# Cut passes, permuted passes and single activation tiles in the feed-forward of a two-layer trunk

## The chip, the cores and the metric

The kernel runs on one core of one Trainium2 chip. The metric is the device time of one execution in microseconds. Three runs of the kernel before took 2742.55, 2743.82 and 2744.37 us; their median is 2743.82 us. One further execution was taken with the hardware profiler.

## The reference

A trunk of two layers works on 256 tokens of 2048 features in float32. Each layer has a mixer and a feed-forward, both with an RMS norm ahead and a residual behind. The mixer of layer 0 is differential attention, that of layer 1 a gated DeltaNet. The change lies in the feed-forward, which is the same in both layers:

```python
def conv_ffn(h, w_up, conv_w, conv_b, w_down):
    u = causal_dwconv(h @ w_up, conv_w) + conv_b
    val, gate = jnp.split(u, 2, axis=-1)
    return (jax.nn.silu(gate) * val) @ w_down

for i in range(DEPTH):                    # DEPTH = 2
    h = rms_norm(x, mixer_norm[i])
    x = x + (diff_attention(h, ...) if i == 0 else gated_deltanet(h, ...))
    x = x + conv_ffn(rms_norm(x, ffn_norm[i]), ffn_w_up[i], ffn_conv_w[i], ffn_conv_b[i], ffn_w_down[i])
```

`w_up` is 2048 x 11008 and `w_down` 5504 x 2048 in each layer. The causal convolution has three taps.

## The kernel before

Activations are kept transposed, features on the 128 partitions and the 256 tokens along the free dimension. `self.x` holds the residual as 16 tiles of 128 x 256, `self.h` the normed input of the next product.

Every large product is done in three passes. A float32 operand is split into a high part, rounded to the fp32r type, and a low part, the rest. ScalarE makes the high part of a weight chunk (L78), VectorE the low part (L79), both in `weights`; activations are split likewise in `norm_tile`, `split` and elsewhere, and stand as a tile of two halves, `a[:, 0]` high and `a[:, 1]` low. The three passes are high weights by high activations (L104, called h below), low weights by high activations (L105, m), and high weights by low activations (L106, l). They add into one PSUM bank.

`dense` (L90) makes one block of 256 output features: two columns c of 128, 16 or more contraction steps k, three passes for each pair of k and c, each a matmul of 128 x 128 weights by 256 tokens. The weights come in chunks of four k (CK = 4), 512 KB each, by a DMA from SP into `raw` (four buffers), and from there into `whi` and `wlo` (three buffers each). Within a chunk k runs outside c; in the last chunk of a block c runs outside k. After each chunk `tick` lets background generators (the norm's sum, attention scores, DeltaNet steps) issue their own instructions, so that their matmuls stand in TensorE's queue between those of `dense`. `dense_tok` (L125 to L127) is the variant with 512 columns, used for values and gates.

The feed-forward (`ffn`) runs 43 blocks j of the up projection, each with 16 k, so 96 passes a block and 4128 in all. Block j holds 128 value and 128 gate features. The block's sums go through `merge` (L112), the convolution, SiLU and the product on VectorE and ScalarE, and are split into the activation tile `ac` of block j. Then `project` runs eight blocks of the down projection with 43 k each, 2064 passes, whose activations are the `ac` tiles. At the start of each feed-forward, `norm_stat` is the one background generator: it adds matmuls of the plain float32 type, of 256 columns (L167) and one column (L169), near the start, and multiplies the inverse norm in at `merge`. Later no other matmul stands among the passes of a feed-forward.

Tiles come from pools in the order of their first allocation, rounded to 32 bytes. The constants' pool holds `h0` to `h15`, 2048 bytes each, and is followed by the pool of the weight buffers; the pools of attention, feed-forward and DeltaNet follow and replace each other. In the kernel before, three tiles carry unused columns at their ends: `dist` 72, `fcols` 64 and `con` 64. Modulo 512 bytes, all activations that `dense` reads (`h`, `ac` of attention, `ac` of the feed-forward, `oc` of the DeltaNet) then start at 160, and all weight buffers at 480.

The order of instructions on each engine is set by a scheduler when the program is built. It follows the order of the source closely; waits are put where regions that are read and written overlap.

Of the kernel before, what the change touches and what calls it, by code (L numbers as in the profile page):

```python
# [8 lines left out]
F32 = mybir.dt.float32  # L9
F32R = mybir.dt.float32r  # L10
# [6 lines left out]
P = 128  # L17
T = 256
D = 2048
KD = D // P  # L20
# [5 lines left out]
class Trunk:  # L26
# [8 lines left out]
    def __init__(self, ctx, tc):  # L35
        self.tc, self.nc = tc, tc.nc
        nc = self.nc
        self.bg = deque()
        self.cp = ctx.enter_context(tc.tile_pool(name="cp", bufs=1))
        self.wp = ctx.enter_context(tc.tile_pool(name="wp", bufs=2))  # L40
        self.sp = ctx.enter_context(tc.tile_pool(name="sp", bufs=2))
        self.dps = ctx.enter_context(tc.tile_pool(name="dps", bufs=2, space=PSUM))
        self.mps = ctx.enter_context(tc.tile_pool(name="mps", bufs=4, space=PSUM))
        self.ones = self.cp.tile([P, P], F32, tag="ones", name="ones")
        nc.vector.memset(self.ones, 1.0)
        self.eps = self.cp.tile([P, 1], F32, tag="eps", name="eps")
        nc.vector.memset(self.eps, EPS)
        self.x = self.cp.tile([P, KD, T], F32, tag="x", name="x")
        self.h = [self.cp.tile([P, 2, T], F32R, tag=f"h{k}", name=f"h{k}") for k in range(KD)]
        self.onesr = self.cp.tile([P, P], F32R, tag="onesr", name="onesr")  # L50
        nc.vector.tensor_copy(self.onesr, self.ones)
        self.squares = []
        self.ss = None
        nc.scalar.preload_act_table_set(LNEXP)

    def mp(self):
        return self.mps.tile([P, 512], F32, tag="mp", name="mp")
# [29 lines left out]
    def banks(self):  # L87
        return self.dps.tile([P, 2, 2 * T], F32, tag="ps", name="ps")

    def dense(self, w, kt, acts, tiles=2, lead=0):  # L90

        nc = self.nc
        ps = self.banks()
        for k0, nk in self.chunks(kt, CK, lead):
            hi, lo = self.weights(w[:, k0:k0 + nk, :])
            steps = [(k, c) for k in range(nk) for c in range(tiles)]
            if k0 + nk == kt:
                steps = [(k, c) for c in range(tiles) for k in range(nk)]
            for k, c in steps:
                a = acts(k0 + k)  # L100
                first, last = k0 + k == 0, k0 + k == kt - 1
                s = slice(c * P, (c + 1) * P)
                o = ps[:, c, :T]
                nc.tensor.matmul(o, hi[:, k, s], a[:, 0, :], start=first, stop=False)  # L104
                nc.tensor.matmul(o, lo[:, k, s], a[:, 0, :], start=False, stop=False)  # L105
                nc.tensor.matmul(o, hi[:, k, s], a[:, 1, :], start=False, stop=last)  # L106
            self.tick()
        return ps

# [127 lines left out]
    def ffn(self, w_up, w_down, nj, cols_ap, done, final=False):  # L237

        nc = self.nc
        self.spawn(self.norm_stat())  # L240
        with self.tc.tile_pool(name="fp", bufs=1) as fp:
            cols = fp.tile([P, 8 * nj + 64], F32, tag="fcols", name="fcols")[:, :8 * nj]
            cols = cols.rearrange("p (t h j) -> p t h j", t=4, h=2)
            nc.scalar.dma_start(cols, cols_ap)
            acts = []
            for j in range(nj):
                ps = self.dense(w_up[j], KD, self.h_acts)
                c = []
                u = fp.tile([P, 2, T], F32, tag="u", name="u", bufs=2)
                self.merge(ps, u)  # L250
                for half in range(2):
                    o = fp.tile([P, T], F32, tag=f"cv{half}", name="cv", bufs=2)
                    c4 = [cols[:, t, half, j:j + 1] for t in range(4)]
                    self.conv(o, u[:, half, :], c4[:3], c4[3])
                    c.append(o)
                nc.scalar.activation(c[1], c[1], AF.Silu)
                a = c[0]
                nc.vector.tensor_tensor(a, c[0], c[1], ALU.mult)
                ac = fp.tile([P, 2, T], F32R, tag=f"ac{j}", name="ac")
                self.split(ac, a)  # L260
                acts.append(ac)
            self.project(w_down, nj, lambda k: acts[k], done, final)
# [134 lines left out]
    def gdn(self, w_gate, w_in, w_z, w_out, nb, hb, gate_ap, const_ap, hot_ap, conv_col, ng, done):  # L397
# [7 lines left out]
        nc, tc, mp = self.nc, self.tc, self.mp  # L405
# [3 lines left out]
        gv = 2 * gh  # L409
        with tc.tile_pool(name="gd", bufs=1) as gd:  # L410
            self.spawn(self.norm_stat())
            con = gd.tile([P, 384 + 64], F32, tag="con", name="con")[:, :384]
            nc.sync.dma_start(con, const_ap)
            ident, mask, triu = con[:, :P], con[:, P:T], con[:, T:]
            hot = gd.tile([64, nv], F32, tag="hot", name="hot")
# [15 lines left out]
            def lin(ps):  # L431
                u = gd.tile([P, 2, T], F32, tag="u", name="u", bufs=2)
                self.merge(ps, u)
                return u

            def convs(u, tiles):
                c = gd.tile([P, 2, T], F32, tag="cv", name="cv", bufs=4)
                for i in range(2):
                    self.conv(c[:, i, :], u[:, i, :], [conv_col(t, tiles[i]) for t in range(4)], None)
                nc.scalar.activation(c, c, AF.Silu)  # L440
                return c
# [126 lines left out]
            def to_tokens(c, vt, g, ready):  # L568
                yield
                yield  # L570
                p = mp()
                for t in range(2):
                    for i in range(2):
                        nc.tensor.transpose(p[:, (2 * t + i) * P:(2 * t + i + 1) * P], c[:, i, t * P:(t + 1) * P], ident)  # L574
                nc.scalar.copy(vt[:, :, g:g + 2, :], p.rearrange("p (t v c) -> p t v c", t=2, v=2))
                ready.append(g)
# [70 lines left out]
            def out(b, acts):  # L647
                for blk in range(KD // 2):
                    ps = self.dense(w_out[b * (KD // 2) + blk], 2 * hb, lambda k: self.await_(acts, k))
                    self.add_out(blk, ps, done if b == nb - 1 else None)  # L650
# [4 lines left out]
            for b in range(nb):  # L655
                heads = range(b * hb, (b + 1) * hb)
                cc = gd.tile([P, 32, 32], F32, tag="s4", name="Cc", bufs=3)
                nc.gpsimd.memset(cc, 0.0)
                lqs, inv, acts, zts, vts = [], [], [], {}, {}
                groups = [range(i, i + gh) for i in range(0, hb, gh)]  # L660
                plan = [("k", i) for i in range(hb)] + [("v", 0)] + [("z", g) for g in range(len(groups))]
                for op, i in plan + [("v", i) for i in range(1, hb)]:
                    if op == "k":
                        hq = heads[i]
                        c = convs(lin(self.dense(w_in[hq * 2], KD, self.h_acts)), (hq, nq + hq))
                        self.spawn(keys(hq, c, cc, 2 * i, lqs))
                        if i == hb - 1:
                            self.spawn(invert(cc, lqs, inv))
                    elif op == "z":
                        gr = groups[i]  # L670
                        zt = zts[i] = gd.tile([P, 2, gv, P], F32, tag="vz", name="zt", bufs=4)
                        ps = self.dense_tok(w_z[heads[gr[0]] // 2], KD, self.h_acts)
                        for t in range(2):
                            nc.scalar.activation(zt[:, t].rearrange(flat), ps[:, t, :], AF.Silu,
                                                 scale=self.rstdc[:, t:t + 1])
                    else:
                        gi = i // gh
                        gr = groups[gi]
                        if i == gr[0]:
                            vt = gd.tile([P, 2, gv, P], F32, tag="vz", name="vt", bufs=4)  # L680
                            ready = []
                            self.spawn(group(gi, gr, lqs, inv, vt, ready, zts, acts))
                        hq = heads[i]
                        c = convs(lin(self.dense(w_in[hq * 2 + 1], KD, self.h_acts)),
                                  (2 * nq + 2 * hq, 2 * nq + 2 * hq + 1))
                        self.spawn(to_tokens(c, vt, 2 * (i - gr[0]), ready))
                if pend:
                    out(*pend)
                pend = (b, acts)
            out(*pend)  # L690

    def gates(self, gd, pg, nv, gp, ident, triu, res):
# [199 lines left out]
```

## Time and profile before

| | |
|---|---|
| median of three runs | 2743.82 us |
| lowest, highest | 2742.55, 2744.37 us |
| the profiled execution, its own time | 2744.12 us |
| its span, first to last instruction | 2742.3 us |
| granted TensorE clock, mean | 0.999 |
| matmul instructions in it | 22352, as many weight loads |
| passes of the two feed-forwards (L104, L105, L106) | 2 x 6192 |
| bytes moved by DMA | 481.62 MB, 176 GB/s on the mean |

The page gives for each engine the busy time and its share of the span. PE is TensorE's matmuls, PEld its weight loads, which overlap the matmuls; DVE is VectorE, ACT ScalarE. A matmul's drawn length is modelled and overlaps the next one's, so the time that one matmul costs is the distance between its start and the next start, read from the timeline. A window's row lists, for a stretch of the span, its length and for each engine the busy time and, in brackets, the number of instructions in it. A group's row lists line, engine, operation, the tiles written and read, shapes and count, then busy time and mean of one in ns, then the idle time before them and what ended it.

### The profile page before, as it was taken

The page shows a single profiled execution, that of the slowest core. Times are in us where ns is not written, and L with a number is a line of the kernel's source. Part 1 is how long each engine was busy: PE and PEld are TensorE (multiplying, and loading weights), DVE is VectorE, ACT ScalarE, POOL GpSimd, SP SyncE. Part 2 cuts the span into 40 slices and gives each one's busy share as a digit, 9 for nine tenths or more (in the row PEclk, how much of TensorE's full clock was granted, in tenths as well). Part 3 has the DMA queues.
Part 4 walks back from the last instruction along what each step waited for, and adds up shares of the span by engine and source line. Part 5 has one row for each costly group of instructions (what it writes and reads, how often), then busy time and mean ns, then how long its engine had stood idle before and what let it go on. Part 6 is the DMA issues. An engine that isn't in the chain of part 4 may idle for free.

```text
span 2742.3 us, 53669 instructions
## 1 busy us (share of the span) xinstructions
PE 2728.7 (100%) x22352; PEld 2656.1 (97%) x22352; DVE 1857.5 (68%) x2719; ACT 1457.5 (53%) x1994; POOL 118.4 (4%) x220
## 2 busy tenths in 40 slices
PE   8999999999999999999999999999999999999999
PEld 8998999999999999989989989989999999999999
DVE  7775667666666555688787787688676666665444
ACT  6565655555555444574764664574555555554333
POOL 0000000000000000021011011021000000000000
PEclk9999999999999999999999999999999999999999
DMA  6555555555555556545354454454455555556664
GB/s 214 169 169 169 168 189 185 186 188 188 186 186 189 185 187 187 186 155 177 122 170 140 147 172 144 155 168 157 152 187 186 186 187 188 186 186 193 191 196 151
DMA packets 135396, 481.62 MB, mean 176 GB/s; under 512 B 15344, under 2 KB 18416, under 8 KB 135152
## 3 DMA queue, kind: packets, MB, share of 16 engines
q1 hardware_dynamic: 134000, 475.57, 53.8%
q8 instruction: 175, 2.87, 0.4%
q10 hardware_dynamic: 1152, 2.61, 0.3%
q14 instruction: 69, 0.57, 0.1%
HBM read 476.03 MB, written 2.10 MB: 174 GB/s over the span
## 4 chain that ended last, share of the span: by engine, by line
PE 99%; ACT 0%; DVE 0%; DMA 0%; issue 0%; SPq 0%; DVEq 0%; ACTq 0%
PE ps L105 28%; PE ps L104 27%; PE ps L106 27%; PE ps L125 3%; PE ps L127 3%; PE ps L126 3%; PE mp L595 2%; PE mp L213 1%; PE mp L483 1%; PE mp L538 0%; PE mp L547 0%; PE mp L460 0%; PE mp L559 0%; PE mp L565 0%; PE mp L574 0%; PE mp L482 0%
## 5 line engine op out<-in xcount | busy, mean ns | idle before, releaser
L79 DVE TENSOR_TENSOR wlo<-raw,whi 128x1024 fp32r<-128x1024 f32 (+2 forms) x909 | 1108.5, 1220 | 690.1 <-ACT whi L78 685.4
L78 ACT CAST whi<-raw 128x1024 fp32r<-128x1024 f32 (+2 forms) x909 | 950.8, 1047 | 1091.3 <-PE ps L106 913.1
L104 PE MATMUL ps<-h,whi 128*128 128x256 f32 x4304 | 1208.2, 281 | 9.0 <-ACT h L139 5.3
L105 PE MATMUL ps<-h,wlo 128*128 128x256 f32 x4304 | 1209.1, 281 | 0.5 <-DVE wlo L79 0.4
L106 PE MATMUL ps<-h,whi 128*128 128x256 f32 x4304 | 1207.8, 281 | 0.0
L104 PEld LDWEIGHTS ps<-h,whi 128*128 128x128 f32 x4304 | 820.7, 191 | 11.6 <-ACT h L139 5.3
L105 PEld LDWEIGHTS ps<-h,wlo 128*128 128x128 f32 x4304 | 810.2, 188 | 4.3 <-DVE wlo L79 1.2
L106 PEld LDWEIGHTS ps<-h,whi 128*128 128x128 f32 x4304 | 809.9, 188 | 1.4
L104 PE MATMUL ps<-ac,whi 128*128 128x256 f32 x1632 | 458.4, 281 | 0.0
L105 PE MATMUL ps<-ac,wlo 128*128 128x256 f32 x1632 | 458.3, 281 | 0.0
L106 PE MATMUL ps<-ac,whi 128*128 128x256 f32 x1632 | 458.2, 281 | 0.0
L104 PEld LDWEIGHTS ps<-ac,whi 128*128 128x128 f32 x1632 | 312.2, 191 | 0.0
L105 PEld LDWEIGHTS ps<-ac,wlo 128*128 128x128 f32 x1632 | 307.2, 188 | 0.0
L106 PEld LDWEIGHTS ps<-ac,whi 128*128 128x128 f32 x1632 | 306.2, 188 | 0.0
L125 PE MATMUL ps<-whi,h 128*128 128x512 f32 x384 | 151.7, 396 | 0.0
L127 PE MATMUL ps<-whi,h 128*128 128x512 f32 x384 | 150.8, 393 | 0.0
L126 PE MATMUL ps<-wlo,h 128*128 128x512 f32 x384 | 150.6, 392 | 0.0
L104 PE MATMUL ps<-oc,whi 128*128 128x256 f32 x512 | 145.5, 284 | 0.0
L106 PE MATMUL ps<-oc,whi 128*128 128x256 f32 x512 | 145.0, 283 | 0.0
L105 PE MATMUL ps<-oc,wlo 128*128 128x256 f32 x512 | 144.8, 283 | 0.0
L194 DVE SCALAR_TENSOR_TENSOR cv<-u,fcols,cv 128x255 f32<-128x255 f32 (+1 forms) x344 | 142.8, 478 | 0.0
L112 DVE TENSOR_TENSOR u<-ps,rstd 128x512 f32<-128x512 f32 x118 | 81.4, 690 | 51.0 <-PE ps L106 50.9
(201 smaller groups left out, 2227.1 us busy)
## 6 DMA issues: line engine op xcount, KB each, us to landing
raw<-w_up SPq DMA_DIRECT2D x344, 512.0 KB, 4.3
raw<-w_down SPq DMA_DIRECT2D x160, 512.0 KB, 3.6
raw<-w_in SPq DMA_DIRECT2D x128, 512.0 KB, 4.3
raw<-w_z SPq DMA_DIRECT2D x64, 512.0 KB, 3.8
raw<-w_out SPq DMA_DIRECT2D x64, 512.0 KB, 3.6
raw<-w_qk SPq DMA_DIRECT2D x63, 512.0 KB, 4.0
raw<-w_v SPq DMA_DIRECT2D x32, 512.0 KB, 3.7
raw<-w_o SPq DMA_DIRECT2D x32, 512.0 KB, 4.3
```

The source lines that it names most:

```text
L78: nc.scalar.copy(hi, raw)
L79: nc.vector.tensor_tensor(lo, raw, hi.bitcast(F32), ALU.subtract)
L104: nc.tensor.matmul(o, hi[:, k, s], a[:, 0, :], start=first, stop=False)
L105: nc.tensor.matmul(o, lo[:, k, s], a[:, 0, :], start=False, stop=False)
L106: nc.tensor.matmul(o, hi[:, k, s], a[:, 1, :], start=False, stop=last)
L112: self.nc.vector.tensor_tensor(u, ps[:, :, :T], self.rstd.unsqueeze(1).to_broadcast([P, 2, T]), ALU.mult)
L125: nc.tensor.matmul(ps[:, c, :], ah, hi[:, k, :], start=first, stop=False)
L126: nc.tensor.matmul(ps[:, c, :], ah, lo[:, k, :], start=False, stop=False)
L127: nc.tensor.matmul(ps[:, c, :], al, hi[:, k, :], start=False, stop=last)
L194: nc.vector.scalar_tensor_tensor(out[:, j:], u[:, :T - j], taps[n - 1 - j], out[:, j:], ALU.mult, ALU.add)
L213: last = self.nc.tensor.matmul(out, self.onesr, p[:, j], start=i + j == 0, stop=i + j == n)
L595: nc.tensor.matmul(p[:, v, :], l(v), r[:, v, :], start=i == 0, stop=i == len(terms) - 1)
```

## The change

`dense` takes an order of the three passes and a column at which to cut. In layer 0 (not `final`), every second block has one pass cut: the high pass of k = 1, c = 0 becomes two matmuls, over tokens 0 to w and w to 256, with w = 2, 14, 26, ..., 230 in blocks 1, 3, ..., 39 and 254 in block 41. In layer 1 (`final`), block j takes one of seven orders by j modulo 7: hml, hlm, mhl, HML, hml, lhm, HLM. Lower case means that the three passes of one k and c follow each other in that order; upper case that both c are run for each pass of a k, in all chunks, before the next pass.

The tiles `h0` to `h15` become one tile with eight more columns (32 bytes), and the `ac` tiles of a feed-forward one tile with eight more columns, now allocated ahead of `u` and `cv`. `h` starts at column 0 up to the last output projection of the DeltaNet, where `place(4)` moves its rows by four elements (16 bytes) for layer 1's feed-forward; `ac` starts at column 4 in layer 0 and 0 in layer 1. The 64 unused columns of `con` go.

The built program has 21 matmuls more than before (21,586 in place of 21,565 in the source's counting). On the other engines the same instructions stand in the same order; the counts of matmuls that they wait for are shifted by the added matmuls, and by one or two more where an order lets a weight buffer's last read come earlier. VectorE gets a wait of its own on TensorE in front of some `wlo` writes, where the low weights are now read after the high ones.

```diff
-        self.h = [self.cp.tile([P, 2, T], F32R, tag=f"h{k}", name=f"h{k}") for k in range(KD)]
+        self.hs = self.cp.tile([P, KD * 2 * T + 8], F32R, tag="h", name="h")
+        self.place(0)
...
+    def place(self, d):
+
+        self.h = self.rows(self.hs, KD, d)
+
+    def rows(self, t, n, d):
+
+        return [t[:, d + k * 2 * T:d + (k + 1) * 2 * T].rearrange("p (i t) -> p i t", i=2) for k in range(n)]
...
-    def dense(self, w, kt, acts, tiles=2, lead=0):
+    def dense(self, w, kt, acts, tiles=2, lead=0, order="hml", cut=0):
...
-            for k, c in steps:
+            todo = [(k, c, x) for k, c in steps for x in order.lower()]
+            if order.isupper():
+                todo = [(k, c, x) for k in range(nk) for x in order.lower() for c in range(tiles)]
+            for k, c, x in todo:
                 a = acts(k0 + k)
-                first, last = k0 + k == 0, k0 + k == kt - 1
                 s = slice(c * P, (c + 1) * P)
-                o = ps[:, c, :T]
-                nc.tensor.matmul(o, hi[:, k, s], a[:, 0, :], start=first, stop=False)
-                nc.tensor.matmul(o, lo[:, k, s], a[:, 0, :], start=False, stop=False)
-                nc.tensor.matmul(o, hi[:, k, s], a[:, 1, :], start=False, stop=last)
+                first = k0 + k == 0 and x == order[0].lower()
+                last = k0 + k == kt - 1 and x == order[-1].lower()
+                wt, i = {"h": (hi, 0), "m": (lo, 0), "l": (hi, 1)}[x]
+                edges = [0, cut, T] if cut and (k0 + k, c, x) == (1, 0, "h") else [0, T]
+                for t0, t1 in zip(edges, edges[1:]):
+                    nc.tensor.matmul(ps[:, c, t0:t1], wt[:, k, s], a[:, i, t0:t1], start=first, stop=last)
             self.tick()
...
             acts = []
+            rows = self.rows(fp.tile([P, nj * 2 * T + 8], F32R, tag="ac", name="ac"), nj, 0 if final else 4)
             for j in range(nj):
-                ps = self.dense(w_up[j], KD, self.h_acts)
+                if final:
+                    how = {"order": ("hml", "hlm", "mhl", "HML", "hml", "lhm", "HLM")[j % 7]}
+                else:
+                    how = {"cut": 0 if j % 2 == 0 else min(T - 2, 12 * (j // 2) + 2 if j < 41 else 254)}
+                ps = self.dense(w_up[j], KD, self.h_acts, **how)
...
-                ac = fp.tile([P, 2, T], F32R, tag=f"ac{j}", name="ac")
+                ac = rows[j]
                 self.split(ac, a)
...
-            con = gd.tile([P, 384 + 64], F32, tag="con", name="con")[:, :384]
+            con = gd.tile([P, 384], F32, tag="con", name="con")[:, :384]
...
                 pend = (b, acts)
+            self.place(4)
             out(*pend)
```

## The prediction

> **What bounds the kernel now.** I read the page first: busy shares, clock row, chain.
>
> ```profile
> span 2742.3 us, 53669 instructions
> ...
> PE 2728.7 (100%) x22352; PEld 2656.1 (97%) x22352; DVE 1857.5 (68%) x2719; ACT 1457.5 (53%) x1994; POOL 118.4 (4%) x220
> ...
> PEclk9999999999999999999999999999999999999999
> ...
> PE 99%; ACT 0%; DVE 0%; DMA 0%; issue 0%; SPq 0%; DVEq 0%; ACTq 0%
> ```
>
> TensorE is the chain from end to end, at full clock. So only two things can move the time: the number of matmuls, and the distance from one matmul's start to the next. A busy share hides that distance, because the matmuls overlap: each is drawn 0.28 us long. I therefore took it from the timeline of PE. First the feed-forward of layer 0, then a stretch of the attention; of each, the first and the last row of 25 in a row.
>
> ```profile
> 699.84 0.28 PE L104 MATMUL ps<-h,whi 128*128 128x256 f32 x1
> ...
> 702.67 0.28 PE L104 MATMUL ps<-h,whi 128*128 128x256 f32 x1
> ```
>
> ```profile
> 118.19 0.28 PE L104 MATMUL ps<-h,whi 128*128 128x256 f32 x1
> ...
> 120.91 0.28 PE L104 MATMUL ps<-h,whi 128*128 128x256 f32 x1
> ```
>
> The first pair gives 2.83 us / 24 = 117.9 ns, the second 2.72 us / 24 = 113.3 ns. Same lines, same shapes, same kind of tiles, same clock: the stream has two cadences, 4.5 ns apart (4%). The windows say how long each lasts (the count in brackets is of matmuls; two or three of it began before the window).
>
> ```profile
> core 0: us, PE busy (x), PEclk, DMA share, GB/s
> 108.20:117.00 8.80, 8.80 (x77) 1.00 0.66 213
> 117.90:122.60 4.70, 4.70 (x43) 1.00 0.60 205
> 124.50:131.70 7.20, 7.20 (x66) 1.00 0.36 132
> 424.00:724.00 300.00, 300.00 (x2550) 1.00 0.58 187
> 1256.00:1280.00 24.00, 24.00 (x215) 1.00 0.61 195
> 2050.00:2350.00 300.00, 300.00 (x2549) 1.00 0.58 187
> ```
>
> With two taken off each count: 117 ns in the first row, 115 and 113 in the next two (one head of the attention), 118 in both feed-forwards, 113 in the DeltaNet stretch. The feed-forwards run in the slow cadence throughout; attention and DeltaNet change between both. What switches it shows in the timeline around other kinds of matmul in the stream.
>
> ```profile
> 413.47 0.28 PE L104 MATMUL ps<-h,whi 128*128 128x256 f32 x1
> 413.59 0.59 PE L167 MATMUL mp<-ss,ones 128*128 128x256 f32 x2
> 414.02 0.50 PE L169 MATMUL mp<-ones,ss 128*128 128x1 f32 x4
> 414.39 0.36 PE L105 MATMUL ps<-h,wlo 128*128 128x256 f32 x1
> 414.59 0.28 PE L106 MATMUL ps<-h,whi 128*128 128x256 f32 x1
> 414.70 0.28 PE L104 MATMUL ps<-h,whi 128*128 128x256 f32 x1
> ```
>
> ```profile
> 122.83 0.60 PE L328 MATMUL mp<-qkn 128*128 128x256 f32 x2
> 123.26 0.38 PE L327 MATMUL mp<-qkn 128*128 128x128 f32 x2
> 123.48 0.60 PE L328 MATMUL mp<-qkn 128*128 128x256 f32 x2
> 123.73 0.47 PE L104 MATMUL ps<-h,whi 128*128 128x256 f32 x1
> ...
> 124.50 0.28 PE L106 MATMUL ps<-h,whi 128*128 128x256 f32 x1
> 124.61 0.28 PE L104 MATMUL ps<-h,whi 128*128 128x256 f32 x1
> ```
>
> After the one-column matmuls of the norm the stream goes on at 0.11 to 0.12, and the window from 424 shows that it stayed slow; after the attention scores it settles within six matmuls at 113 ns. So a matmul of another length re-times the stream, and the stream then keeps what it fell into until the next one. Inside the feed-forwards there is no such matmul today.
>
> **The change part by part.** The base is the profiled execution: 2744.1 us, of which 2742.3 are the span. It lies 0.3 us over the median of the runs shown (2743.82). No engine but PE gets another instruction or another order; waits on PE keep their places, with counts shifted by the added matmuls.
>
> *The cut passes (layer 0).* In blocks j = 1, 3, ..., 41 the pass of high weights at k = 1, c = 0 becomes two matmuls of w and 256 - w columns, w = 2, 14, ..., 230 and 254, each with its own weight load: 21 matmuls more, all on the path that sets the end. No row shows an fp32r matmul under 256 columns, so the price is bounded. The lower bound goes by the weight loads:
>
> ```profile
> 414.36 0.19 PEld L105 LDWEIGHTS ps<-h,wlo 128*128 128x128 f32 x1
> 414.47 0.19 PEld L106 LDWEIGHTS ps<-h,whi 128*128 128x128 f32 x1
> ```
>
> Two loads follow each other in 0.11 us where the matmuls are short; two pieces then take 0.22 instead of 0.118, and 21 x 0.10 = 2.2 us. The upper bound: every matmul narrower than 256 here is plain fp32, and those stream slower. From the score rows, 256 columns take 123.26 - 122.83 = 0.43 us, and 128 columns 123.48 - 123.26 = 0.22: the same per column, so any split costs 0.43, 0.31 more than now, and 21 x 0.31 = 6.6 us. A gain is excluded for the pass itself. I take the upper end, since all narrow rows of the trace are of that kind.
>
> By the Trainium skill (TensorE: Matmul & The Clock Gate, section "LDWEIGHTS (loading the stationary operand)") a load takes its 128 columns over 1.2, 107 ns; as an estimate the cuts would cost 21 x (213 - 118) = 2.0 us. The rows above agree with the load's price; they do not say whether a narrow fp32r piece streams at full rate.
>
> *What the cuts do to the cadence.* Each is a re-timing event where there was none, one for every 192 passes (22.6 us). From block 1 on 42 x 96 = 4032 passes of the up projection follow a cut; all fast, they would save 4032 x 4.5 ns = 18 us. In the head shown, two of three stretches are fast; the norm's event ended slow. I take 0.6: minus 10.7 us. Bounds: nothing if every cut falls back to slow, minus 18 if none does. After the last cut stand 2064 passes of the down projection (8 blocks x 43 x 2 x 3) without another event: 9.2 us, one draw. Its second piece has 2 columns, nearest to the one-column rows, which ended slow: I take nothing, and keep minus 9.2 for the range.
>
> *The orders (layer 1).* The passes of the up projection are permuted; no matmul is added, and none changes length, so by the rows above nothing re-times the stream. What could be late is the low half, which two orders want first. The groups in the up projection of layer 1:
>
> ```profile
> L104 PE MATMUL ps<-h,whi 128*128 128x256 f32 x1376 | 386.7, 281 | 0.0
> ...
> L79 DVE TENSOR_TENSOR wlo<-raw,whi 128x1024 fp32r<-128x1024 f32 x172 | 210.7, 1225 | 124.0 <-ACT whi L78 122.9
> L78 ACT CAST whi<-raw 128x1024 fp32r<-128x1024 f32 x172 | 181.3, 1055 | 222.8 <-PE ps L106 189.5 <-ACT cv L192 31.8 <-issue 1.5
> ```
>
> PE never idles, and ScalarE waits 189.5 us for PE to free a buffer: the halves lie finished ahead of their use. Orders that end on a low or high pass shift a buffer's release by one or two passes (0.12 to 0.24 us), inside that wait. Cost nothing; without that cover a chunk would wait for a 1.2 us subtraction. In the last chunk HML lets both halves of the block finish together instead of one after the other; the merge reads both anyway.
>
> *Single tiles and the shift of four elements.* Reads and writes are tracked by region, so no wait is added; `place(4)` sits where the earlier readers of `h` are long done. The 32 bytes added to `h` move every later tile. Modulo 512 bytes, the activation stood 192 behind its weights in all of `dense`; now that is 160 (attention, layer 0 up, DeltaNet), 176 (layer 1 up), 208 (layer 0 down), 448 (DeltaNet's output projection), 192 still in `w_o` and layer 1 down. No row has another distance for these lines, so I bound it by the cadences: 4.5 ns per pass either way. Over the 4128 up passes of layer 1 and the 2064 down passes of layer 0 this is 28 us in each direction, over the whole of both feed-forwards 56. I take nothing: both cadences occur at one distance, so distance alone does not set it.
>
> By the Trainium skill (the same page, "Step-by-step: what each phase is for") weights and moving operand have separate read ports and a load takes no bandwidth from the running matmul; by that, the shift is worth nothing and the two layout rivals below fall away. No run here shows a shift.
>
> Sum: 2744.1 + 6.6 - 10.7 = 2740.0 us.
>
> **The rivals.** (A, the forecast) as above; by its bounds from 2744.1 + 2.2 - 18 - 9.2 = 2719 to 2750.7, mostly 2730 to 2747.
>
> (B, the layout frees a stage) Shifted operands fall into 113 ns in layer 1 or in the shifted half of each layer: 6192 x 4.5 = 28 us more, 2740.0 - 28 = 2712. For it: the fast cadence exists for these very instructions. Against it: the norm's event before layer 1 stays as it is, and it ended slow in both layers.
>
> (C, slower) The mechanism: operands moved off a distance that all four stages shared meet their weight loads worse, in the stages whose distance changed. One step of 4.5 ns on 6192 passes costs 28: 2768. It outweighs the forecast's 4.1 us from 4.1 us / 12384 feed-forward passes = 0.33 ns per pass, so very little suffices. For it: both cadences are slower than the 107 ns which 0.43 / 4 gives for a quarter of the fp32 stream, so something between loads and stream does cost time. Against it: nothing shows that it depends on addresses.
>
> (D, the cuts re-time nothing) Every cut falls back into 118, as the one-column event does: 2744.1 + 6.6 = 2750.7, or 2746.3 at the lower price.
>
> **How the numbers follow.** A 0.38, B 0.20, C 0.30, D 0.12. Within 0.2% means within 5.5 us of 2743.8, about what a measurement can tell from no change. A gives 0.20 faster, 0.16 same, 0.02 slower; B is faster; C slower; D 0.04 same, 0.08 slower. Together 0.40, 0.20, 0.40. The time is A's, 2740.0; A's own range is 2727 to 2750. For 8 in 10 the range reaches B's and C's values, 2712 to 2768.
>
> **What would show it.** Cuts: in layer 0's up projection the distance after each cut, 113 or 118, kept for 192 passes. Price: the distance from the piece's start to the next pass, 0.22 or 0.43. Orders: layer 1 keeps one cadence from the norm's event to the end, without idle time before `wlo`. Layout: the cadence in attention and DeltaNet, which have no cuts. I am wrong in the reason, even at the right time, if the cadence changes inside a block without a cut, or if a third distance appears.

## The result and the profile after

The changed kernel takes 2766.07 us (median of three runs, 2765.43 to 2767.39) against 2743.82 before: a ratio of 1.0083, with a 95% interval of 1.0060 to 1.0106. It is slower by 22 us, where 2740.0 was forecast.

The page of the changed kernel, span and engines:

```profile
span 2765.6 us, 53711 instructions
...
PE 2751.5 (99%) x22373; PEld 2674.1 (97%) x22373; DVE 1858.0 (67%) x2719; ACT 1452.5 (53%) x1994; POOL 117.3 (4%) x220
```

TensorE is still busy from end to end, with 21 matmuls more. At the 118 ns of a pass these are 2.5 us of the 23.3 us by which the span grew; the rest must lie in the distance between matmuls. To see where, take from the timeline of PE the first matmul of each stage. First the kernel before (start, drawn length, engine and line, operation):

```profile
404.99 0.28 PE L104 MATMUL ps<-h,whi 128*128 128x256 f32 x1
...
892.06 0.28 PE L104 MATMUL ps<-ac,whi 128*128 128x256 f32 x1
...
1135.15 0.28 PE L104 MATMUL ps<-h,whi 128*128 128x256 f32 x1
...
2008.20 0.28 PE L104 MATMUL ps<-h,whi 128*128 128x256 f32 x1
...
2495.26 0.28 PE L104 MATMUL ps<-ac,whi 128*128 128x256 f32 x1
```

The same in the changed kernel, where all passes have line 122:

```profile
411.63 0.28 PE L122 MATMUL ps<-h,whi 128*128 128x256 f32 x1
...
902.18 0.28 PE L122 MATMUL ps<-ac,whi 128*128 128x256 f32 x1
...
1148.14 0.28 PE L122 MATMUL ps<-h,whi 128*128 128x256 f32 x1
...
2034.49 0.28 PE L122 MATMUL ps<-h,whi 128*128 128x256 f32 x1
...
2527.67 0.28 PE L122 MATMUL ps<-ac,whi 128*128 128x256 f32 x1
```

Differences of these rows, with the span as the last end, give the stages:

| stage | before, us | after, us | difference | distance modulo 512, before and after |
|---|---|---|---|---|
| attention | 404.99 | 411.63 | +6.6 | h 192, 160 |
| layer 0 up (21 cuts) | 487.07 | 490.55 | +3.5 | 192, 160 |
| layer 0 down | 243.09 | 245.96 | +2.9 | 192, 208 |
| DeltaNet | 873.05 | 886.35 | +13.3 | h 192, 160; oc 192, 448 |
| layer 1 up (seven orders) | 487.06 | 493.18 | +6.1 | 192, 176 |
| layer 1 down | 247.04 | 237.93 | -9.1 | 192, 192 |

20 of the 23 us lie in attention and DeltaNet, which have neither a cut nor an order. Inside these two stages the loss lies in the passes that read `h`: from first to last start, attention's output projection (distance 192 before and after) took 93.59 us in both kernels, and the DeltaNet's last output projection (192, now 448) 111.18 and 111.19. The only stage that won, layer 1 down, is one whose distance between activation and weights stayed. Windows of the changed kernel (length, busy time, and in brackets the matmuls; two or three began before):

```profile
950.00:1050.00 100.00, 100.00 (x842) 1.00 0.59 185
2100.00:2200.00 100.00, 100.00 (x841) 1.00 0.56 185
...
2560.00:2660.00 100.00, 100.00 (x885) 1.00 0.66 206
```

With two taken off, layer 0 down and layer 1 up run at 119 ns a pass, a spacing that no stage of the kernel before keeps; layer 1 down runs at 113.3, without a cut.

### The profile page after: what moved, and what is told of

It is laid out like the page before. It is cut to its first block, busy times and chain, and to the rows that moved or that the text cites. A ratio compares the mean times of both kernels' runs of the same rounds, so it can differ in the third digit from the quotient of the medians.

```text
span 2765.6 us, 53711 instructions
## 1 busy us (share of the span) xinstructions
PE 2751.5 (99%) x22373; PEld 2674.1 (97%) x22373; DVE 1858.0 (67%) x2719; ACT 1452.5 (53%) x1994; POOL 117.3 (4%) x220
## 4 chain that ended last, share of the span: by engine, by line
PE 99%; ACT 0%; DVE 0%; DMA 0%; issue 0%; SPq 0%; DVEq 0%; ACTq 0%
PE ps L122 82%; PE ps L141 3%; PE ps L142 3%; PE ps L143 3%; PE mp L616 2%; PE mp L229 1%; PE mp L504 1%; PE mp L559 0%; PE mp L568 0%; PE mp L481 0%; PE mp L580 0%; PE mp L586 0%; PE mp L595 0%; DMA raw<-w_qk 0%; PE mp L503 0%; PE mp L660 0%
## 5 line engine op out<-in xcount | busy, mean ns | idle before, releaser
L122 PE MATMUL ps<-h,whi 128*128 128x256 f32 (+1 forms) x8629 | 1535.3, 282 | 9.2 <-ACT h L155 5.2
L122 PEld LDWEIGHTS ps<-h,whi 128*128 128x128 f32 x8629 | 1316.7, 189 | 13.3 <-ACT h L155 5.2
L122 PE MATMUL ps<-ac,whi 128*128 128x256 f32 x3264 | 571.0, 280 | 0.0
L122 PEld LDWEIGHTS ps<-ac,whi 128*128 128x128 f32 x3264 | 497.7, 188 | 0.0
L122 PE MATMUL ps<-oc,whi 128*128 128x256 f32 x1024 | 188.0, 284 | 0.0
L122 PEld LDWEIGHTS ps<-oc,whi 128*128 128x128 f32 x1024 | 159.0, 190 | 0.1
L122 PEld LDWEIGHTS ps<-oc,wlo 128*128 128x128 f32 x512 | 98.0, 191 | 0.2
L208 ACT ACTIVATE cv<-u,fcols 128x256 f32<-128x256 f32 x172 | 93.7, 592 | 0.1
L210 DVE SCALAR_TENSOR_TENSOR cv<-u,cols,cv 128x254 f32<-128x254 f32 (+2 forms) x192 | 91.0, 517 | 3.2 <-ACT cv L206 2.9
L143 PEld LDWEIGHTS ps<-whi,h 128*128 128x128 f32 x384 | 72.1, 188 | 17.2
```

The source lines that it names most:

```text
L122: nc.tensor.matmul(ps[:, c, t0:t1], wt[:, k, s], a[:, i, t0:t1], start=first, stop=last)
L143: nc.tensor.matmul(ps[:, c, :], al, hi[:, k, :], start=False, stop=last)
L208: nc.scalar.activation(out, u, AF.Identity, bias=bias, scale=taps[n - 1])
L210: nc.vector.scalar_tensor_tensor(out[:, j:], u[:, :T - j], taps[n - 1 - j], out[:, j:], ALU.mult, ALU.add)
```

## The experiments

Nine kernels, each measured beside the kernel before. Counts of 885, 852 and 841 in a window of 100 us stand for 113.3, 117.8 and 119.2 ns a pass, as read from the starts of the passes.

**1. The distances put back** (`e1_distance_back`). From the changed kernel, keeping cuts, orders and single tiles:

```diff
-        self.hs = self.cp.tile([P, KD * 2 * T + 8], F32R, tag="h", name="h")
+        self.hs = self.cp.tile([P, KD * 2 * T], F32R, tag="h", name="h")
...
-            rows = self.rows(fp.tile([P, nj * 2 * T + 8], F32R, tag="ac", name="ac"), nj, 0 if final else 4)
+            rows = self.rows(fp.tile([P, nj * 2 * T], F32R, tag="ac", name="ac"), nj, 0)
...
-            con = gd.tile([P, 384], F32, tag="con", name="con")[:, :384]
+            con = gd.tile([P, 384 + 64], F32, tag="con", name="con")[:, :384]
...
-            self.place(4)
+            self.place(0)
```

> The changed kernel with the cuts, the orders and the single tiles kept, but every address of the kernel before: no extra columns, no shift by four elements, the 64 unused columns of con back, so that activation minus weights is 192 bytes modulo 512 in all passes of dense. Theory (distance): attention, DeltaNet and layer 1 (orders) run as before, layer 1 at 117.8 ns per pass through the up projection, FFN 0 alternates between 113.3 and 117.8 after the cuts and never leaves these two; 2743.8 + 21 x 0.10 = 2746 us if every cut falls back to slow, down to 2746 - 27 = 2719 if all fall to fast. Rival (cuts and orders are what cost): stays at 2760 to 2768 us, with distances other than 113.3 and 117.8 in layer 1.

Measured: 2730.53 us, ratio 0.9951 (0.9935 to 0.9968). So with the old addresses the change would have been faster. Its windows, in layer 0 up, layer 0 down and layer 1 up:

```profile
500.00:600.00 100.00, 100.00 (x885) 1.00 0.62 193
900.00:1000.00 100.00, 100.00 (x851) 1.00 0.60 186
2050.00:2150.00 100.00, 100.00 (x852) 1.00 0.59 186
```

Layer 1, with all seven orders, is back at 117.8: the orders do nothing. Layer 0 up runs at 113.3. Over the whole trace, the passes behind each of the first 20 cuts (2 to 230 columns) have 113.3, and those behind the last one (254 and 2) have 117.8, through the down projection. Only the first and the last of these cuts moved the stream, from 117.8 to 113.3 and back; the 19 between left it at 113.3. Timeline around the cut at 98 columns (x3 is a low pass and the two pieces):

```profile
592.94 0.28 PE L122 MATMUL ps<-h,wlo 128*128 128x256 f32 x1
593.05 0.46 PE L122 MATMUL ps<-h,whi 128*128 128x256 f32 x3
593.35 0.32 PE L122 MATMUL ps<-h,wlo 128*128 128x256 f32 x1
593.50 0.40 PE L122 MATMUL ps<-h,whi 128*128 128x256 f32 x2
593.74 0.28 PE L122 MATMUL ps<-h,wlo 128*128 128x256 f32 x1
```

Two triples of passes take 593.74 - 592.94 = 0.80 us instead of 6 x 0.1133 = 0.68: a cut costs 0.12 us. The same rows of the changed kernel:

```profile
606.59 0.28 PE L122 MATMUL ps<-h,wlo 128*128 128x256 f32 x1
...
607.40 0.28 PE L122 MATMUL ps<-h,wlo 128*128 128x256 f32 x1
```

0.81 against 6 x 0.1173 = 0.70, so 0.11. The other cuts of the two kernels cost 0.09 to 0.14 us by their starts, whatever the width. That is near the lower bound of the prediction, 0.10, and far from the 0.31 that was taken.

**2. The layout alone** (`e2_layout_only`). From the changed kernel, without cuts and orders:

```diff
-                if final:
-                    how = {"order": ("hml", "hlm", "mhl", "HML", "hml", "lhm", "HLM")[j % 7]}
-                else:
-                    how = {"cut": 0 if j % 2 == 0 else min(T - 2, 12 * (j // 2) + 2 if j < 41 else 254)}
-                ps = self.dense(w_up[j], KD, self.h_acts, **how)
+                ps = self.dense(w_up[j], KD, self.h_acts)
```

> The changed kernel with neither cuts nor orders: only the single tiles, the shifts and the missing columns of con. Theory (distance): attention and DeltaNet as in the changed kernel (406 and 886 us), layer 1 up at 119.3 ns per pass, layer 0 down at 119.2, layer 0 up in one of the cadences of distance 160 throughout (117.3, 118.7 or 120.1 ns: 484, 490 or 496 us); 2758 to 2772 us. Rival (cuts and orders are what cost): back to 2742 to 2748 us.

Measured: 2760.48 us, ratio 1.0061 (1.0046 to 1.0076). The layout alone costs 17 us; cuts and orders add some 5. Its windows in layer 0 up, layer 0 down and layer 1 up:

```profile
440.00:540.00 100.00, 100.00 (x854) 1.00 0.58 187
...
950.00:1050.00 100.00, 100.00 (x841) 1.00 0.59 183
2100.00:2200.00 100.00, 100.00 (x841) 1.00 0.58 184
```

Layer 1 counts the same 841 with one order as with seven. Layer 0 up runs at 117.3 without cuts; in the changed kernel each cut at this distance put the stream at 117.3 or 118.7, nine of them at 117.3 and twelve at 118.7, and never at 113.3. So at distance 160 there was nothing for the cuts to win.

**3. Everything moved, distance kept** (`e3_all_moved`). Is it the distance, or where the weights start?

```diff
-        self.eps = self.cp.tile([P, 1], F32, tag="eps", name="eps")
+        self.eps = self.cp.tile([P, 9], F32, tag="eps", name="eps")[:, :1]
```

> The kernel before with 32 unused bytes ahead of everything, so that activations and weights both move by 32 bytes and their distance stays 192; the weights then start at 0 modulo 512, as in the changed kernel. Theory (distance between the two decides): within 3 us of 2743.8, both feed-forwards at 117.8 ns. Rival (the start address of the weights decides): 2755 us or more, with 117 to 120 ns spacings as in the changed kernel.

Measured: 2719.0 us (two runs, 2718.81 and 2719.20), ratio 0.9911 (0.9891 to 0.9931). The start address of the weights is not the cause: they start at 0 modulo 512, as in the changed kernel, and no third spacing appears. But the time was missed by 25 us, since layer 0 fell into the fast cadence by itself (windows in layer 0 up, layer 0 down, layer 1 up):

```profile
450.00:550.00 100.00, 100.00 (x885) 1.00 0.61 194
930.00:1030.00 100.00, 100.00 (x885) 1.00 0.63 193
2050.00:2150.00 100.00, 100.00 (x852) 1.00 0.58 187
```

At this distance, then, both cadences are open to the same code, and a shift of all tiles by 32 bytes was enough to change which one the norm's matmuls leave behind in layer 0, but not in layer 1. Why, no run here tells.

**4. Distance 128** (`e4_h_distance_128`). What is the period?

```diff
-        self.onesr = self.cp.tile([P, P], F32R, tag="onesr", name="onesr")
+        self.onesr = self.cp.tile([P, P + 16], F32R, tag="onesr", name="onesr")[:, :P]
```

> The kernel before with 64 unused bytes between h and the weights: h stands at 128 instead of 192 modulo 512, ac and oc keep 192. Theory with a period of 64 bytes: h passes know only 113.3 and 117.8 ns; the time is 2716 to 2746 us by which of the two the feed-forwards catch. Rival (192 and 448 are special, a period of 128 or 256): h passes show other spacings with a mean over 118 ns, and the time is 2755 us or more.

Measured: 2757.57 us, ratio 1.0051 (1.0031 to 1.0072). The period of 64 bytes falls: layer 0 up (h at 128) is slower than any stage above, layer 0 down (ac still at 192) is fast.

```profile
450.00:550.00 100.00, 100.00 (x836) 1.00 0.57 184
950.00:1050.00 100.00, 100.00 (x885) 1.00 0.63 192
```

Layer 1 up, also at 128, ran at 118.7, so this distance too allows more than one spacing. What 192 and 448 share, and 128 lacks, is the remainder 64 modulo 128; but they also share 192 modulo 256, and this run cannot tell the two periods apart.

**5. A scan of distances** (`e6_scan`). From the kernel before, with the weights starting at another column in each block of the up projections:

```diff
-            t = self.wp.tile([P, CK * T], dt, tag=tag, name=tag, bufs=bufs)
-            return t[:, :nk * n].rearrange("p (k n) -> p k n", n=n)
+            d = self.shift if dt == F32R else 0
+            t = self.wp.tile([P, CK * T + (32 if dt == F32R else 0)], dt, tag=tag, name=tag, bufs=bufs)
+            return t[:, d:d + nk * n].rearrange("p (k n) -> p k n", n=n)
...
+                self.shift = (31 - j if final else j) % 32
                 ps = self.dense(w_up[j], KD, self.h_acts)
+                self.shift = 0
```

> The kernel before with the weight buffers 32 columns wider and, in block j of an up projection, weights starting j columns (4 j bytes) further in layer 0 and 31 - j in layer 1, so that the distance of h to the weights runs through 64 - 4 j modulo 128 bytes. Theory (distance modulo 128 decides, 64 is the good one): blocks near 64 modulo 128 at 113.3 or 117.8, distances 0 and 32 at 117 to 120, 16, 48 and 80 at about 119.2; both layers give the same mean at the same distance, except where one distance has two cadences. Rival (distance modulo 128 is not what decides): the two layers disagree block by block, or all blocks stay at 117.8. The time itself is 2740 to 2765 us.

The buffers are 128 bytes wider, so neighbouring ones of the same tile lie 128 bytes apart modulo 512; a block uses several of them, and a distance is given modulo 128.

Measured: 2720.99 us (one run); the time was missed, because both down projections caught 113.3. Windows of 9 us inside blocks: in layer 0 the distances modulo 128 are 0, 108, 64, 52 and 44, in layer 1 108, 0, 44 and 52.

```profile
583.00:592.00 9.00, 9.00 (x78) 1.00 0.56 182
640.00:649.00 9.00, 9.00 (x75) 1.00 0.55 179
766.00:775.00 9.00, 9.00 (x82) 1.00 0.62 192
799.50:808.50 9.00, 9.00 (x82) 1.00 0.59 187
822.00:831.00 9.00, 9.00 (x77) 1.00 0.60 181
2107.00:2116.00 9.00, 9.00 (x75) 1.00 0.58 179
2164.00:2173.00 9.00, 9.00 (x78) 1.00 0.58 180
2289.00:2298.00 9.00, 9.00 (x78) 1.00 0.58 181
2312.00:2321.00 9.00, 9.00 (x81) 1.00 0.58 187
```

In these rows the layers agree within a matmul although the distances come in opposite order; over all blocks, visits to one distance differ by up to 2.2 ns, at 76 by 3.1. From the starts of the whole blocks, without the first of each layer, which holds the norm's matmuls: 113.5 to 114.0 ns at 52, 113.6 and 113.8 at 64, 113.4 to 116.5 at 76, and 116.6 to 124.1 at the other 29 distances, the worst at 108.

The trace holds something else. Outside the up projections the weights start where they did, at 64 modulo 128, but in the wider buffers, and there the slow cadence does not last. The rows are of the attention, behind one of its own matmuls (lines 106 to 108 are the three passes here): the first, the 36th and the 45th pass.

```profile
189.75 0.28 PE L106 MATMUL ps<-h,whi 128*128 128x256 f32 x1
...
193.90 0.28 PE L108 MATMUL ps<-h,whi 128*128 128x256 f32 x1
...
194.92 0.28 PE L108 MATMUL ps<-h,whi 128*128 128x256 f32 x1
```

The first 35 spacings are 4.15 us / 35 = 118.6 ns, the next nine 1.02 us / 9 = 113.3, with no other matmul between. No stretch over 116.5 ns at this distance, as a mean of six, is longer than 36 passes here; in the kernel before, attention's output projection held 117.8 for over 700 and layer 0's feed-forward for over 6000. The DeltaNet's last output projection took 111.2 us in the kernel before, in the changed one and in runs 1 to 4, and 109.0 here. So the width of the buffers counts as well as the distance modulo 128.

**6. Two cuts, and four** (`e5_two_cuts`, `e7_four_cuts`). From the kernel before, at its distance of 192: one cut in block 1 of each feed-forward, then two more in projections that ran slow.

```diff
+                edges = [0, cut, T] if cut and (k0 + k, c) == (1, 0) else [0, T]
+                for t0, t1 in zip(edges, edges[1:]):
+                    nc.tensor.matmul(o[:, t0:t1], hi[:, k, s], a[:, 0, t0:t1], start=first, stop=False)
-                nc.tensor.matmul(o, hi[:, k, s], a[:, 0, :], start=first, stop=False)
...
-                ps = self.dense(w_up[j], KD, self.h_acts)
+                ps = self.dense(w_up[j], KD, self.h_acts, cut=98 if j == 1 else 0)
```

and in the second kernel also

```diff
-            self.add_out(b, self.dense(w[b], kt, acts), done)
+            self.add_out(b, self.dense(w[b], kt, acts, cut=98 if kt == KD and b == 2 else 0), done)
...
-                    ps = self.dense(w_out[b * (KD // 2) + blk], 2 * hb, lambda k: self.await_(acts, k))
+                    ps = self.dense(w_out[b * (KD // 2) + blk], 2 * hb, lambda k: self.await_(acts, k),
+                                    cut=98 if b == nb - 1 and blk == 1 else 0)
```

> The kernel before, with its addresses, and one cut in each feed-forward: block 1, first high pass of k = 1, c = 0, at 98 columns, behind the norm's matmuls. Theory (at distance 192 a cut sets the stream to 113.3 ns and it stays until the next matmul of another length): from block 1 on, 42 x 96 + 2064 = 6096 passes of each layer save 4.44 ns, 27.1 us, and each cut costs 0.1: 2743.1 - 54 = 2689 us, plus or minus 3. Rival (the many cuts of the run with the addresses put back were needed, or layer 1 does not respond): 2714 to 2745 us.

> The two cuts and two more of the same kind: in block 2 of attention's output projection (some 660 slow passes follow) and in block 1 of the DeltaNet's last output projection (some 330 slow passes follow). Theory: another (660 + 330) x 4.44 ns - 0.2 us = 4.2 us less than with two cuts, 2685 us. Rival (those stretches are slow for another reason, or the norm's matmuls re-time what follows): no change against two cuts, or the feed-forward behind falls back.

Measured: 2689.65 us, ratio 0.9799 (0.9785 to 0.9814), and 2683.73, ratio 0.9779 (0.9763 to 0.9796). Two more matmuls in 22,352 take off 55 us. The two further cuts bring 5.9 us where 4.2 was expected; by the starts, the two projections account for 3.7 of it (91.20 in place of 93.59 us, 109.85 in place of 111.18). Windows of the first, in layer 0 up and down and layer 1 up and down:

```profile
450.00:550.00 100.00, 100.00 (x885) 1.00 0.64 194
900.00:1000.00 100.00, 100.00 (x884) 1.00 0.66 196
2000.00:2100.00 100.00, 100.00 (x884) 1.00 0.65 194
2500.00:2600.00 100.00, 100.00 (x885) 1.00 0.69 201
```

**7. Distance 52, and 76, throughout** (`e8_distance_52`, `e9_distance_76`). The wider buffers of the scan, with one start for all weights; no cut.

```diff
+        self.shift = 3
```

and `self.shift = 29` in the second.

> The kernel before with weights that start three columns (12 bytes) further in their buffers everywhere, so that activation minus weights is 52 modulo 128 in all passes; no cuts, no orders. In the scan the blocks at 52 ran at 113.4 ns in all three visits, whatever came before, and never at 117.8. Theory (at 52 the slow cadence does not exist): the 15900 slow passes of the kernel before save 4.4 ns each, 70 us; 2743.8 - 70 = 2674 us, at most some 10 us more where the 512-column products lose. Rival (52 has both cadences like 64 and the scan happened to catch the fast one): one or both feed-forwards at 117 or more, 2690 to 2750 us.

> The same with 29 columns (distance 76 modulo 128). In the scan 76 gave 113.4, 114.4 and 116.2, so both cadences or a changing one. Theory: distance 76 is good but not safe; between 2674 and 2745 us, with stretches at 113 and at another spacing. Rival (76 behaves like 52): 2674 us, no other spacing.

Measured: 2677.13 us, ratio 0.9758 (0.9742 to 0.9774), and 2740.50, ratio 0.9989 (0.9980 to 0.9999). At 52, layer 0 up and layer 1 down:

```profile
450.00:550.00 100.00, 100.00 (x885) 1.00 0.65 194
...
2500.00:2600.00 100.00, 100.00 (x885) 1.00 0.69 201
```

Every long stretch of the trace runs at 113.3, after each kind of interruption: the slow cadence did not last anywhere, and no cut is needed. Since neighbouring buffers lie 128 bytes apart, this one trace runs at 52, 180, 308 and 436 modulo 512, all fast: that speaks for a period of 128 bytes, and against 256. But the kernel differs from the one before in two things, the 12 bytes and the wider buffers. By the trace of the scan the wider buffers alone may keep 64 fast; they were not run with all weights unshifted, so it is not shown which of the two brings the 66 us.

The kernel at 76 has the same wide buffers. There the up projections ran at 118.3 (847 in a window of 100 us) and the down projections, for the most part, at 113.3:

```profile
450.00:550.00 100.00, 100.00 (x847) 1.00 0.61 186
950.00:1050.00 100.00, 100.00 (x885) 1.00 0.67 195
```

So wide buffers alone do not make every distance near 64 fast: between two kernels that differ in nothing but where the weights start, 52 and 76, lie 63 us.

## Why the prediction was wrong, step by step

- *The bound.* Right: TensorE's spacing sets the time, and no other engine came near.
- *The shift of the tiles.* This step failed. The prediction bounded it by 4.5 ns a pass and took nothing, "both cadences occur at one distance, so distance alone does not set it". That inference was wrong: that one distance allows two cadences does not mean that other distances allow the same two. Runs 1 and 2 show it: the layout alone costs 17 us, and without it the change is 13 us faster than the kernel before. The bound itself held: 9.0 us on 6192 shifted feed-forward passes are 1.5 ns a pass. The third distance between starts, which the prediction named as the sign of a wrong reason, appeared: 119.2 ns at 176 and 208, 118.7 at 160. The rival C named the mechanism and the sign; its price of 28 us counted the shifted feed-forward passes, where 9 us were lost, and not attention and DeltaNet, where 20 were, nor the 9 us that layer 1 down won. That its 2768 lies so near the measured 2766 is luck.
- *The ports.* The Trainium skill (TensorE: Matmul & The Clock Gate, "Step-by-step: what each phase is for") gives weights and moving operand separate read ports, a load taking no bandwidth from the matmul. By that, the prediction said, the shift would be worth nothing. In these runs the spacing of the same matmuls changes from 113.3 to 124.1 ns with where one operand lies relative to the other, and the measurement decides. Why it does is open: no run here tells whether the two reads meet or something else is at work.
- *What the cuts do to the cadence.* The principle held for the buffers of the kernel before (an event of another length re-times the stream, which then keeps its cadence; in the wider buffers of run 5 it did not keep the slow one). 0.6 of the passes fast was too low for the distance before: there the passes behind 20 of 21 cuts ran at 113.3. (0.6 of 4032 passes at 4.5 ns is 10.9 us; the 10.7 of the sum goes by 4.44 ns.) But the step was worked out at a distance that the change itself abolishes. At 160 the cuts chose between 117.3 and 118.7, and lost 3 us, besides their own price, against the 117.3 of run 2.
- *The last cut.* Right in run 1: with two columns last it ended slow where the fast cadence was open. It is one cut; that its width is the reason was not tried.
- *The price of a cut.* Wrong end of the bounds: some 0.11 us, 2.2 us in all, as the rows of two weight loads gave it, and not 6.6. Pieces of fp32r narrower than 256 columns do not fall to the rate of plain fp32.
- *The orders.* Right: nothing, in both layouts. Layer 1 up takes the same time with seven orders as with one, at 192 (487.0 us from first to last start) and at 176 (493.1).
- *The gain of layer 1 down* (9 us) was in no step. It kept its distance of 192, was entered from a stream with other spacings, and fell into the fast cadence. The down projections did so in all six such entries (changed kernel, run 2, both layers of runs 4 and 5); why is not shown.
- *The sum again.* The forecast had 0 for the shift, +6.6 for the price and -10.7 for the cadence. Measured were +17 by run 2, +2.2 and +3, which is the 22 us.

## What to carry to other kernels

Where TensorE is bound by a stream of equal matmuls, read the distance between their starts and not their busy time, stage by stage; two stages with the same shapes and different spacings may be a gain to be had. Choose the addresses of moving operand and weights together, scan their distance within 128 bytes in one kernel, and take one at which only the fast spacing occurs, before trying to knock the stream from one cadence into another. Run the place found throughout the kernel before trusting it: 76 ran at 113.4 ns in one block of the scan, and slow when all blocks had it. A change that resizes any early tile moves everything behind it, so layout and the edit under study need separate runs.

## What the runs showed of the hardware

- The spacing of 128x256 fp32r matmuls, each with its own weight load, ranged from 113.3 to 124.1 ns at full clock (0.999 granted) with the distance between activation and weights (run 5). Of the 32 distances modulo 128 bytes only 52, 64 and 76 had 113.3; between 52 and 76, in kernels alike otherwise, lie 63 us (2677.13 and 2740.50).
- At a distance of 64 modulo 128, in the buffers of the kernel before, the stream has two steady cadences, 113.3 and 117.8 ns, each kept for thousands of passes; one split matmul (0.1 us) moved it from one to the other, saving 27 us in each feed-forward.
- In buffers 128 bytes wider, at the same distance of 64, the slow cadence went back to 113.3 ns by itself within 36 passes (run 5).
